# Both even output projections ahead of the odd layer, with its normed rows kept in memory as 16-bit parts

## The chip, the cores and the metric

The kernel runs on one core of one Trainium2 chip. The metric is the device time of one execution in microseconds; several executions are timed and their median is compared. One further execution is taken with the hardware profiler, and all rows below come from that one.

## The reference

One step of a two-layer decoder over 2048 prompt rows and 32 sample rows (8 sequences of 4), 1024 columns wide. Layer 0 ("even") runs HGRN2 and forgetting attention side by side, layer 1 ("odd") is a gated linear attention (GLA). Cut to what matters:

```python
for l in range(2):                       # even, then odd
    h = rmsnorm(x, norm[l])
    if l == 0:
        out = concat([o_hgrn, o_fox]) @ w_out_even     # each o gated by silu
    else:
        q, k, v, g, r = split(h @ w_in_odd, [512, 512, 1024, 1024, 16])
        log_f = log_sigmoid(r @ w_gate + b_gate) / 16
        o, s = gated_linear_chunked(q, k, v, log_f, s0)   # 4 heads
        out = (head_rmsnorm(o) * silu(g)) @ w_out_odd
    x = x + out
y = rmsnorm(x, final_norm)
```

So the odd layer's norm needs whole rows of x, that is all four column slices of the even output projection and the residual.

## The kernel before

The prompt is worked on in two halves of 1024 rows; half 0 also carries the 32 sample rows. The activations that TensorE reads stand in one tile, `act`: two 16-bit parts (a high part and the rest) of 1024 x 1056 numbers, columns being rows of x. Every projection multiplies three times (high by high, high by rest, rest by high: `mm3`, L549 to 553). There is only one `act`, so a half's input is written over the columns of what was there before, tile by tile as the matmuls have read them.

A projection is a list of *units* of some 256 weight columns. Each unit has four steps besides its matmuls: fetch (L329), measure, scale and split of its weights. `staged` (L1168) runs units a to b and slips the steps of the units one to three ahead between a unit's tile groups; it is `dense` in the odd phase. A unit of the output projection (`out_units`, L1756) ends each pair of tiles by adding the residual to the PSUM result on VectorE. An odd head has three units: Cv (values, and for head 0 also 16 gate columns), Cqk (queries, gate, keys) and Cg (the silu path). Cv of head 0 runs tile by tile, and for each tile it turns the gate columns on TensorE two tiles later (`flip`, L1837; `rh`, `rt` on VectorE before it, `prT` in PSUM). `lin_attn` is one head's recurrence: short matmuls in chains with VectorE and GpSimd. `mux` interleaves two generators by their stated costs.

The phase of the odd layer (`phase_odd`, L1909) runs, in order:

1. even output projection of half 0, units 0 to 3. Its rows x1 were loaded whole into SBUF (`row_tiles`) and are stored whole after unit 3 (L1784).
2. `start(0)`: while unit 3 runs, `handed` (L506) takes its tile pairs as they finish, through `norm_rows` (L460): square with sum on ScalarE (L481), reciprocal root, gain and scale (L485, L489), split into high part (L486, L490) and rest (L487, L491) in the staging tile `xhl`, and a DMA transpose of `xhl` into `act` (L498). Cv of head 0 starts behind it.
3. Cqk and Cg of head 0, then the recurrences of heads 0 to 2, each beside the units of the next head.
4. recurrence 3 beside `second()`: half 1's even outputs `yT` loaded and split into `act` (`y_to_act`, `y_pieces` L1710, split on L1730 to 1735), its output projection with residual slices loaded and stored through `xo` (L1771 to 1776), and `start(1)`: norm of half 1 from rows read back (three quarters from memory, the last columns copied from `xo` on L1931) and Cv of head 0 of half 1.
5. the same for half 1, then the odd output projections of both halves and the final norm.

All loads and stores of this phase go through SyncE's queue (SP), which takes them one after the other. The order of each engine's instructions, SP's too, is fixed when the program is built: a planner runs through the program with estimated times and puts next what is ready, so a later line can come ahead of an earlier one. `issue_after` puts instructions behind a given one on the same engine. Tiles of one tag share a number of buffers: `yr` two (8 KB a partition), `c2` four (shared by `xo`, the squares and the recurrence), weight raws `wr` three, split weights `w` three, PSUM `pj` three.

Of the kernel before, what the change touches and what calls it, by code (L numbers as in the profile page):

```python
# [8 lines left out]
F32 = mybir.dt.float32  # L9
F32R = mybir.dt.float32r  # L10
BF16 = mybir.dt.bfloat16
F16 = mybir.dt.float16
# [7 lines left out]
P = 128  # L20
# [89 lines left out]
def drain(g):  # L110
    for _ in g:
        pass
# [11 lines left out]
class Kern:  # L124
    def __init__(self, ctx, tc, ins, outs):
        self.ctx, self.tc, self.nc = ctx, tc, tc.nc
        self.i, self.o = ins, outs
        self.loaded, self.last_cols = {}, {}


    def consts(self):
# [27 lines left out]
        self.x1d = dp.tile([NTOK, D], F32, name="x1d")  # L159

# [344 lines left out]
    @staticmethod  # L505
    def handed(groups, first, last):  # L506


        for t in range(len(groups) + 1):
            c = next(last, None)  # L510
            if c:
                yield c
            if t >= 3:
                c = next(first, None)
                if c:
                    yield c
            if t < len(groups):
                groups[t][0]()
            if t:
                groups[t - 1][1]()  # L520
        yield from last
        yield from first
# [508 lines left out]
    def phase_even(self):  # L1031
# [4 lines left out]
        with pool("act", side="right") as ap, pool("w", side="right") as w0, pool("wl", side="right") as wp1, \  # L1036
# [5 lines left out]
            nrm = Pool(n0, {"th": 1, "nss": 4, "rs_t": 4, "rs_r": 4})  # L1042
            self.scales2, self.ready, self.fsc, self.logit, self.v_undo = {}, {}, {}, {}, {}
# [124 lines left out]
    def staged(self, us, a, b, beside=None, late=False):  # L1168
# [3 lines left out]
        def step(u, n):  # L1172
            if u < len(us):
                with ExitStack() as st:
                    if beside and n == 1 and u < 4:

                        st.enter_context(self.tc.issue_after(self.last_v.ins))
                    if late and n:
                        st.enter_context(self.tc.issue_after(self.last_lo.ins))
                    self.ready[u] = us[u][0][n]()  # L1180

        for j in range(a, b):
# [6 lines left out]
            if late:  # L1189
                todo = [[], [], [], [], [(j + 3, 0)], [(j + 2, 1)], [(j + 2, 2), (j + 2, 3)]]  # L1190
# [565 lines left out]
    def out_units(self, hf, layer, act, wpool, wp, pps, x2=None, done=None):  # L1756
# [4 lines left out]
        def mk(u):  # L1761
# [3 lines left out]
            def ev(ps, g, cnt, m):  # L1765
                c0 = self.ttiles(hf)[g][0]
                c = undo[-1 if m < P else 0][:m]
                if x2 is None:
# [4 lines left out]
                    if u == 3:  # L1773
                        self.last_cols[c0] = t
# [20 lines left out]
    def odd_half(self, hf, act, wpool, wp, pps, S):  # L1795
# [18 lines left out]
        def mk_v(h):  # L1814
            width = 272 if h == 0 else 256

            def run(W):
# [5 lines left out]
                def ev(ps, g, cnt, m):  # L1823
                    c = undo(f"Cv{h}")[:m]
                    if m == P:
                        nc.scalar.activation(v[h][:, g : g + cnt], ps[:, :, :256], AF.Copy, scale=c)
                    else:
                        nc.scalar.activation(vs[h], ps[:, 0, :256], AF.Copy, scale=c)
# [80 lines left out]
    def phase_odd(self):  # L1909
# [4 lines left out]
        with pool("act2", side="right") as ap, pool("w2", side="right") as w0, pool("yr2", side="right") as y0, \  # L1914
# [11 lines left out]
            def get_x1(hf):  # L1926
                def get(c0, m):
                    t = wp.tile([P, HALF + TS], F32, tag="c4", name=f"x1r{hf}{c0}")[:, :D]

                    nc.sync.dma_start(t[:m, :768], self.rows(hf, c0, m, False)[:, :768])  # L1930
                    nc.gpsimd.tensor_copy(t[:m, 768:], self.last_cols[c0 // 256 * 256][:m, c0 // P % 2])  # L1931
                    return t
                return get

# [12 lines left out]
            x1, x2 = [], []  # L1947
# [9 lines left out]
            def dense(a, b, **kw):  # L1957
                return self.staged(units, a, b, **kw)

            def layer(hf):  # L1960
                drain(dense(16 * hf + 5, 16 * hf + 7))
                for h in range(3):
                    drain(mux(lins[hf](h), LIN_O[hf], dense(16 * hf + 3 * h + 7, 16 * hf + 3 * h + 10), 66000.0))

            def start(hf, get):
                def stage():
                    t = wpool.tile([P, KT, 256], F32, tag="yr", name=f"xhl{hf}").rearrange("p k t -> p (k t)")
                    t = t.bitcast(F16).rearrange("p (j x d) -> p j x d", j=2, x=2)
                    return [t[:, 0], t[:, 1]]

                grow = self.gain_row(wp.tile([P, D], F32, tag="gn", name=f"grow{hf}"), i["norm_odd"][0], self.sx_odd)
                return self.handed(self.norm_rows(wp, act, hf, get, stage, grow),
                                   dense(16 * hf + 4, 16 * hf + 5, late=True), dense(16 * hf + 3, 16 * hf + 4))
# [13 lines left out]
            self.ready, self.sam = {}, None  # L1987
# [38 lines left out]
            drain(mux(lins[0](3), LIN3_A, second(), 130000.0))  # L2026
            layer(1)

# [23 lines left out]
            def third():  # L2052
                self.y_to_act(0, 1, act, wpool)
                yield from dense(32, 36)
# [65 lines left out]
```

## Time and profile before

| | |
|---|---|
| median of 3 executions | 2390.0 us |
| lowest, highest | 2389.28, 2394.76 us |
| the profiled execution | 2395.67 us |
| its span, first to last instruction | 2393.9 us |
| mean granted TensorE clock in it | 0.983 |
| moved by DMA in the span | 331.51 MB, mean 138 GB/s |
| read from and written to HBM | 243.88 and 71.11 MB |

The span starts with the first instruction; times in the views are microseconds from there. The even layer's projections and recurrences take the first part, the forgetting attention the second, and the odd phase begins at 1301.9. A row of the view by stretches gives, after its length, the busy time and number of instructions of each engine, the mean granted clock of TensorE, the mean busy share of the 16 DMA engines and the rate. A row of waits reads: who waited, for whom, microseconds in total, times, longest. A row of groups reads: line, engine, operation, output and inputs, shapes, count, then busy time in all and mean nanoseconds of one, then the engine's idle time just before them and what ended it. Buffer numbers are left out of names.

### The profile page before, as it was taken

What the parts mean: (1) busy time and instruction counts of PE and PEld (TensorE: products, weight loads), DVE (VectorE), ACT (ScalarE), POOL (GpSimd) and SP (SyncE); (2) the same over time, 40 slices, a digit from 0 to 9 for tenths busy, and PEclk for the clock granted to TensorE, in tenths of its full rate; (3) what the DMA queues carried; (4) which work ended last, traced back from release to release, by engine and by line L of the source; (5) the groups of instructions that cost most, each with busy time, mean ns of one, the idle gap of its engine ahead of it and who ended that gap; (6) DMA issues with size and microseconds to landing.
All of it is one profiled execution on the core that took longest, in us unless ns stands there. A gap on an engine that the chain in (4) does not pass through costs nothing. (4 is left out here: it accounts for less than half of the span.)

```text
span 2393.9 us, 58155 instructions
## 1 busy us (share of the span) xinstructions
PE 2279.4 (95%) x23124; PEld 1617.8 (68%) x23124; DVE 1409.6 (59%) x3256; ACT 1093.6 (46%) x2379; POOL 795.3 (33%) x858
## 2 busy tenths in 40 slices
PE   6999999999999989999999989999999899999998
PEld 5677668855655866655447867677678566666887
DVE  7566567435764547567666463665675445557554
ACT  5334354232433236466676354544543435545333
POOL 2233334112212235144466341432452322322223
PEclk9999999999999999999999999999999999999999
DMA  6231335855531276776865491222255712115453
GB/s 198 63 88 58 98 108 156 202 143 147 155 101 64 87 245 194 266 240 211 263 199 183 141 225 56 68 77 71 69 164 160 176 45 66 43 59 159 153 187 153
DMA packets 347906, 331.51 MB, mean 138 GB/s; under 512 B 90241, under 2 KB 291522, under 8 KB 347634
## 3 DMA queue, kind: packets, MB, share of 16 engines
q1 hardware_dynamic: 346130, 323.27, 44.4%
q8 instruction: 182, 2.98, 0.5%
q0 software_dynamic: 1504, 4.52, 0.5%
q14 instruction: 90, 0.74, 0.1%
HBM read 243.88 MB, written 71.11 MB: 132 GB/s over the span
## 5 line engine op out<-in xcount | busy, mean ns | idle before, releaser
L553 PE MATMUL pt_o<-w_o,act 128*128 128x256 f16 x1024 | 282.0, 275 | 4.1 <-DVE act L1735 4.1
L551 PE MATMUL pt_o<-w_o,act 128*128 128x256 f16 x1024 | 282.2, 276 | 1.4 <-ACT sg1C L607 1.4
L552 PE MATMUL pt_o<-w_o,act 128*128 128x256 f16 x1024 | 281.9, 275 | 1.4 <-POOL w_o L355 1.4
L551 PEld LDWEIGHTS <-act 128*128 128x128 f16 x2304 | 228.3, 99 | 44.0 <-issue 6.5
L553 PEld LDWEIGHTS <-act 128*128 128x128 f16 x2304 | 228.2, 99 | 39.3 <-DVE act L1735 4.9
L552 PEld LDWEIGHTS <-act 128*128 128x128 f16 x2304 | 228.3, 99 | 33.3 <-issue 2.1
L551 PE MATMUL pt_Cv<-w_Cv,act 128*128 128x256 f16 (+1 forms) x512 | 144.0, 281 | 7.8 <-DMA act<-xhl 4.1
L552 PE MATMUL pt_Cv<-w_Cv,act 128*128 128x256 f16 (+1 forms) x512 | 143.9, 281 | 0.0
L553 PE MATMUL pt_Cv<-w_Cv,act 128*128 128x256 f16 (+1 forms) x512 | 143.9, 281 | 0.0
L717 POOL TENSOR_TENSOR kA<-kA,fA 128x512 f32<-128x512 f32 (+1 forms) x56 | 79.6, 1421 | 186.8 <-PE gl_A L683 138.3
L1343 ACT ACTIVATE L<-L,nm,kc 128x512 f32<-128x512 f32 (+3 forms) x160 | 118.2, 741 | 37.3 <-DVE nm L1341 33.3
L717 POOL TENSOR_TENSOR kC<-kC,fC 128x512 f32<-128x512 f32 (+1 forms) x56 | 81.5, 1455 | 151.2 <-PE gl_C L683 105.6
L1351 POOL TENSOR_SCALAR L<-L,nm 128x512 f32<-128x512 f32 (+3 forms) x160 | 99.2, 635 | 62.8 <-DVE nm L1347 22.1
L1378 ACT ACTIVATE th<-pt 128x512 f16<-128x512 f32 (+3 forms) x159 | 80.4, 527 | 62.0 <-PE pt L1371 61.1
L1379 DVE TENSOR_TENSOR tl<-pt,th 128x512 f16<-128x512 f32 (+3 forms) x159 | 94.6, 609 | 22.3 <-ACT th L1378 21.3
L1371 PE MATMUL pt<-ident,L 128*128 128x128 f32 x544 | 92.2, 282 | 6.5 <-POOL L L1351 3.7
L1371 PEld LDWEIGHTS pt<-ident,L 128*128 128x128 f32 x544 | 67.6, 145 | 33.4 <-DVE tl L1379 8.9
L1495 PEld LDWEIGHTS pkt<-ident,pgcache_fox_k 128*128 128x128 f32 x512 | 58.3, 143 | 43.2 <-issue 25.9
L1495 PE MATMUL pkt<-ident,pgcache_fox_k 128*128 128x128 f32 x512 | 75.9, 281 | 6.7 <-DVE kts L1499 4.6
L551 PE MATMUL pt_Av<-w_Ai,act 128*128 128x256 f16 x256 | 71.1, 278 | 0.5 <-ACT act L546 0.5
L552 PE MATMUL pt_Av<-w_Ai,act 128*128 128x256 f16 x256 | 70.8, 277 | 0.4 <-DVE w_Ai L348 0.4
L553 PE MATMUL pt_Av<-w_Ai,act 128*128 128x256 f16 x256 | 71.0, 277 | 0.0
(965 smaller groups left out, 6691.9 us busy)
## 6 DMA issues: line engine op xcount, KB each, us to landing
pgcache_fox_k<-in_cache_fox_k SPq DMA_DIRECT2D x128, 256.0 KB, 4.2
pgcache_fox_v<-in_cache_fox_v SPq DMA_DIRECT2D x128, 256.0 KB, 4.0
yr<-yT SPq DMA_DIRECT2D x16, 1024.0 KB, 5.9
wr_Aqf<-in_w_in_even SPq DMA_DIRECT2D x64, 128.0 KB, 3.7
wr_o<-in_w_out_even SPq DMA_DIRECT2D x32, 256.0 KB, 4.1
wr_Cv<-in_w_in_odd SPq DMA_DIRECT2D x32, 256.0 KB, 3.4
wr_Cqk<-in_w_in_odd SPq DMA_DIRECT2D x64, 128.0 KB, 2.4
wr_Cg<-in_w_in_odd SPq DMA_DIRECT2D x32, 256.0 KB, 4.3
```

Of the source, the lines that this page charges most:

```text
L551: nc.tensor.matmul(ps, lh[0], rh[0], start=first, stop=False)
L552: nc.tensor.matmul(ps, lh[0], rh[1], start=False, stop=False)
L553: return nc.tensor.matmul(ps, lh[1], rh[0], start=False, stop=last)
L717: nc.gpsimd.tensor_tensor(kv[:, :, 0], kv[:, :, 0], t1.to_broadcast([P, nb, w]), ALU.mult)
L1343: self.last_exp = nc.scalar.activation(lt[:, :w], lt[:, :w], AF.Exp, bias=nm[:, 0:1], scale=ib, accum_out=nm[:, 2 + j : 3 + j])
L1351: nc.gpsimd.tensor_scalar(lt[:, :w], lt[:, :w], nm[:, 1:2], 2.0**14, ALU.mult, ALU.mult)
L1371: nc.tensor.transpose(pt[:, w : w + P], rows[b][s // 4][0][:, (s % 4) * P : (s % 4 + 1) * P], self.ident)
L1378: nc.scalar.activation(th[:, a:w], pt[:, a:w], AF.Copy),
L1379: nc.vector.tensor_tensor(tl[:, a:w], pt[:, a:w], th[:, a:w], ALU.subtract)))
L1495: nc.tensor.transpose(pk[:, j * P : (j + 1) * P], pgs[j][:, h * P : (h + 1) * P], self.ident)
```

## The change

The four units of half 1's even output projection move from the middle of the odd phase to right behind those of half 0; the units are renumbered (0 to 3 and 4 to 7 the even output projections, 8 to 19 the odd layer of half 0, 20 to 31 that of half 1, then 32 to 39). Both now add the residual in slices (`xo`). Half 1's `yT` is split into `act` behind unit 3, with its first two loads ahead of that unit.

The norm becomes a stream of its own, `norm_store`: rows are read back from x1d, squared, multiplied by the gain, split, and the two 16-bit parts are stored to a new tensor in memory, `xs`, of 2080 rows of 2048 numbers. Half 0's runs beside units 4 to 7, half 1's beside recurrences 0 to 2. `norm_fetch` then transposes `xs` by DMA into `act`, the sample tile first, right before Cv of head 0 of each half. The weights of the unit three ahead are fetched just before it, and `staged` leaves that fetch out later (`early`). Recurrence 3 of half 0 runs beside head 0 of half 1. The weight steps of `staged` are put behind the last eviction of Cv of head 0 on ScalarE (`last_ev`), where `late` put them behind the last rest part. `third()` loads the first two pieces of y ahead of its splits.

```diff
+        self.xs = dp.tile([NTOK, 2 * D], F16, name="xs")
...
+    def norm_store(self, pool, hf, tiles, gain):
+        todo = self.few_first(self.ttiles(hf))
+        fly = {}
+        def load(x):
+            c0, n = todo[x]
+            fly[x] = [y[:n] for y in tiles(c0)]
+            dc = T if c0 >= HALF else hf * HALF + c0
+            nc.sync.dma_start(fly[x][0], self.x1d[dc : dc + n])
+        def norm(x):
+            (c0, n), xt = todo[x], fly[x][0]
...
+            nc.scalar.activation(sq[:n], xt, AF.Square, accum_out=ss[:n])
+            fly[x].append(self.rstd(pool, ss[:n], [n, 1], D, f"n{c0}"))
+            nc.gpsimd.tensor_tensor(xt, xt, gain[:n], ALU.mult)
+        def split(x):
+            (c0, n), (xt, t, r) = todo[x], fly.pop(x)
...
+            nc.scalar.activation(t[:, 0], xt, AF.Copy, scale=r)
+            nc.vector.scalar_tensor_tensor(t[:, 1], xt, r, t[:, 0], ALU.mult, ALU.subtract)
+            nc.sync.dma_start(self.xs[dc : dc + n], t.rearrange("p x d -> p (x d)"))
+        for x in range(len(todo) + 2):
+            if x > 1:
+                split(x - 2)
+            if x < len(todo):
+                load(x)
+            if 0 < x <= len(todo):
+                norm(x - 1)
+            yield 1000
+
+    def norm_fetch(self, act, hf):
...
+        for c0, n in self.few_first(self.ttiles(hf)):
+            dc = T if c0 >= HALF else hf * HALF + c0
+            self.nc.sync.dma_start_transpose(act.both[:, :, :, c0 : c0 + n].rearrange("p x k t -> p (x k) t"),
+                                             self.xs[dc : dc + n])
...
-    def staged(self, us, a, b, beside=None, late=False):
+    def staged(self, us, a, b, beside=None):
-            if u < len(us):
+            if u < len(us) and (n or u not in self.early):
...
-                    if late and n:
-                        st.enter_context(self.tc.issue_after(self.last_lo.ins))
+                    if self.last_ev is not None:
+                        st.enter_context(self.tc.issue_after(self.last_ev.ins))
...
-                nc.sync.dma_start(t[:m, :768], self.rows(hf, c0, m, False)[:, :768])
-                nc.gpsimd.tensor_copy(t[:m, 768:], self.last_cols[c0 // 256 * 256][:m, c0 // P % 2])
...
             for hf in range(2):
-                units += self.out_units(hf, 0, act, wpool, wp, pps, None if hf else x1)
+                units += self.out_units(hf, 0, act, wpool, wp, pps)
+            for hf in range(2):
                 us, lin = self.odd_half(hf, act, wpool, wp, pps, S)
...
-            x1 += row_tiles(0, True, self.last_load)
             with tc.issue_after(self.last_y.ins):
                 drain(dense(0, 3))
-            drain(start(0, lambda c0, n: x1[c0 // P]))
-            layer(0)
-            def second():
-                self.y_to_act(1, 0, act, wpool)
-                yield from dense(16, 19)
-                yield from start(1, get_x1(1))
-            drain(mux(lins[0](3), LIN3_A, second(), 130000.0))
-            layer(1)
+            grow = self.gain_row(wp.tile([P, D], F32, tag="gn", name="grow"), i["norm_odd"][0], self.sx_odd)
+            pieces = load(self.y_pieces(1, 0, act, wpool))
+            drain(dense(3, 4))
+            split(pieces)
+            def prep(hf):
+                def tiles(c0):
+                    t = wpool.tile([P, KT, 256], F32, tag="yr", name=f"x1r{hf}{c0}").rearrange("p k t -> p (k t)")
+                    return t[:, :D], t[:, D:].bitcast(F16).rearrange("p (x d) -> p x d", x=2)
+                return self.norm_store(wp, hf, tiles, grow)
+            drain(mux(prep(0), 11500.0, dense(4, 8), 84000.0))
+            fetched(11)
+            self.norm_fetch(act, 0)
+            drain(dense(8, 11))
+            drain(mux(prep(1), 10000.0, three(0, 11), 240000.0))
+            fetched(23)
+            self.norm_fetch(act, 1)
+            drain(recur(0, 3, 20))
+            drain(three(1, 23))
```

`three(hf, a)` runs recurrences 0 to 2 of a half, each beside three units from a on; `recur` is one of them; `fetched(u)` issues the weight fetch of unit u and notes it in `early`; `load` and `split` here issue the first two loads of the pieces of y, and the splits with the remaining loads.

More of the change, by code (lines that the diff above doesn't have):

```diff
@@ L127, in __init__ @@
         self.i, self.o = ins, outs
-        self.loaded, self.last_cols = {}, {}
+        self.loaded = {}
     def consts(self):
@@ L2052, in third @@
             def third():
-                self.y_to_act(0, 1, act, wpool)
+                pieces = load(self.y_pieces(0, 1, act, wpool))
+                self.sam = None
+                split(pieces)
                 yield from dense(32, 36)
```

71 lines of the change are left out of this document (31 added, 40 removed).

## The prediction

> **What bounds the kernel now.** First the page's head: TensorE (PE) is busy in 95% of the span, so a gain can only be time in which it waits or runs slowly.
>
> ```profile
> span 2393.9 us, 58155 instructions
> PE 2279.4 (95%) x23124; PEld 1617.8 (68%) x23124; DVE 1409.6 (59%) x3256; ACT 1093.6 (46%) x2379; POOL 795.3 (33%) x858
> ```
>
> Then the sums over stretches. The bounds are where the first matmul of a stage starts. In order: even output projection of half 0, its first unit alone, the first odd unit (Cv0) of half 0, the rest of head 0, heads 1 to 3 beside recurrences 0 to 2, then in one stretch recurrence 3, the even output projection of half 1 and Cv0 of half 1, then the rest of that head, heads 1 to 3 of half 1, and all that follows.
>
> ```profile
> core 0: us, PE busy (x) PEld busy (x) DVE busy (x) ACT busy (x) POOL busy (x), PEclk, DMA share, GB/s
> 1301.90:1390.20 88.30, 86.91 (x843) 76.40 (x840) 38.78 (x69) 39.72 (x70) 30.73 (x25) 1.00 0.60 191
> 1301.90:1323.00 21.10, 21.10 (x199) 18.74 (x200) 8.45 (x17) 13.55 (x27) 6.96 (x8) 1.00 1.05 368
> 1390.20:1429.30 39.10, 30.33 (x254) 22.48 (x255) 25.45 (x55) 19.55 (x32) 16.40 (x11) 0.90 1.02 229
> 1429.30:1475.40 46.10, 45.14 (x356) 29.27 (x353) 13.25 (x23) 26.05 (x44) 5.46 (x4) 0.98 0.26 75
> 1475.40:1746.40 271.00, 262.24 (x3183) 196.31 (x3182) 167.11 (x328) 134.23 (x298) 100.69 (x85) 1.00 0.24 74
> 1746.40:1898.30 151.90, 136.81 (x1458) 114.19 (x1457) 93.43 (x167) 59.74 (x122) 60.72 (x56) 0.94 0.63 176
> 1898.30:1941.50 43.20, 42.90 (x260) 19.86 (x258) 10.99 (x15) 21.82 (x31) 5.44 (x4) 1.00 0.19 54
> 1941.50:2184.80 243.30, 240.62 (x2661) 160.71 (x2652) 133.89 (x257) 121.03 (x255) 71.41 (x63) 1.00 0.20 63
> ```
>
> A unit alone takes 21.1 us with PE busy throughout. Two stretches fall off: 39.1 us for one unit at a granted clock of 0.90, and the 151.9 us at 0.94. Both hold a handoff from the even output projection to the odd layer. What PE waited for in the two:
>
> ```profile
> PE pt_Cv L551 <- DMA act<-xhl: 3.3, 1, 3.3
> PE prT L1839 <- DVE rt L1835: 3.0, 1, 3.0
> PE pS_Cv L595 <- DVE sam_Cv L590: 2.0, 1, 2.0
> ```
>
> ```profile
> PE pt_Cv L551 <- DVE rh L1833: 3.2, 1, 3.2
> PE prT L1839 <- DVE rt L1835: 3.0, 2, 1.9
> PE st_C L551 <- ACT vp_C L788: 2.2, 1, 2.2
> PE gl_C L683 <- DVE qC L637: 2.0, 1, 2.0
> PE prT L1839 <- DVE rst_n L405: 1.9, 1, 1.9
> PE gl_C L683 <- DVE qC L716: 1.8, 1, 1.8
> ```
>
> The norm of the last rows, its split and its DMA transposes stand between the last even matmul and the first odd one, and the norm's work on DVE delays Cv0's own small steps. Each wait is followed by a stretch of slow clock, which is why the clock column falls: 0.10 of 39.1 us is 3.9 us, 0.06 of 151.9 us is 9.1 us.
>
> **The work without the waits.** I rebuild both stretches from undisturbed durations. Cv0 has the 192 matmuls of an output unit with 272 columns for 256: 21.1 x 272/256 = 22.4 us. It also turns its small gate columns on PE, once a tile:
>
> ```profile
> L1839 PE MATMUL prT<-ident,rt 128*80 128x128 f32 x15 | 4.5, 301 | 8.0 <-DVE rt L1835 6.0 <-DVE rst_n L405 1.9
> ```
>
> Nine of 0.30 us are 2.7 us. A group of sample rows is some 0.8 us (88.3 less four times 21.1 leaves 3.9 us for three groups and two short waits); two lie in the first stretch, and I allow 1 us for the next unit's first matmuls, which already run there. So 22.4 + 2.7 + 1.6 + 1 = 27.7 us of 39.1: **11.4 us to gain**.
>
> Recurrence 3: a head beside a recurrence takes 271.0/3 = 90.3 us, its matmuls alone 21.1 + 0.8 + 46.1 + 1 = 69.0, so the recurrence adds 21.3 us. After the change the 151.9 us become four output units alone, 84.4 us, and recurrence 3 beside head 0 of half 1: 21.3 + 22.4 + eight turns, 2.4, with the other 43.2 us unchanged. 84.4 + 46.1 = 130.5: **21.4 us to gain**. Together 32.8 us.
>
> **What the change adds.** (1) Between the two output projections half 1's y is split into `act` columns that unit 3 is still reading. The trace has this seam once, between the odd output projections (2295.5 on), where PE waited for the low parts and then ran at half clock for 3.4 us:
>
> ```profile
> PE pt_o L553 <- DVE act L1735: 4.1, 3, 1.8
> ```
>
> ```profile
> 2311.90:2315.30 3.40, 3.14 (x15) 2.24 (x16) 3.40 (x5) 1.05 (x5) 1.85 (x2) 0.51 0.47 161
> ```
>
> That is 4.1 + 1.7 = 5.8 us. The new seam has its first two loads issued a unit earlier and some subtractions on POOL, so it may cost nothing; I take 5.8, the only row. Bounds 0 and 5.8.
>
> The Trainium skill ("TensorE: Matmul & The Clock Gate", Part 1) says that the clock falls after at least one idle window of about 3.4 us. This trace does not agree: three waits of at most 1.8 us each brought a half-clock stretch. By the rule the seam would cost 4.1 us and the forecast would be 1.7 us lower.
>
> (2) The norm of each tile of half 0 now runs beside units 4 to 7, that of half 1 beside recurrences 0 to 2. A tile costs, from these rows:
>
> ```profile
> L481 ACT ACTIVATE nsq<-x1r 128x1024 bf16<-128x1024 f32 x8 | 8.4, 1045 | 1.7 <-POOL x1r L1931 1.7
> L489 POOL TENSOR_TENSOR x1r<-x1r,grow 128x1024 f32<-128x1024 f32 x4 | 9.8, 2453 | 5.4 <-ACT nsq L481 5.4
> L490 ACT ACTIVATE xhl<-x1r,rsr_n 128x1024 f16<-128x1024 f32 x4 | 4.6, 1149 | 8.5 <-POOL rsr_n L407 8.5
> L491 DVE SCALAR_TENSOR_TENSOR xhl<-x1r,rsr_n,xhl 128x1024 f16<-128x1024 f32 x4 | 5.1, 1276 | 0.0
> ```
>
> ACT 2.2, DVE 1.3, POOL 2.5 us. Beside units 4 to 7 nine tiles are 20, 12 and 22 us in 84 us on engines that the first unit above uses for 7 to 14 us of its 21: hidden. Uncovered, a tile's chain would be 1.0 + 2.5 + 1.1 + 1.3 us and a memory round trip. Beside the recurrences it is some 4, 6 and 7 us a head. The third head already carries about 5 more on each of the three than the second:
>
> ```profile
> 1565.70:1655.80 90.10, 87.40 (x1070) 65.47 (x1060) 54.01 (x108) 43.44 (x98) 31.80 (x27) 1.00 0.23 72
> 1655.80:1746.40 90.60, 87.48 (x1069) 65.46 (x1062) 59.03 (x112) 47.55 (x104) 37.05 (x31) 1.00 0.26 79
> ```
>
> Its time is 0.4 us over the mean of the other two, (271.0 - 90.6)/2 = 90.2. So 0.4 a head, 1.2 us. Bounds 0 and 9.4: the three waits of recurrence 3 above (2.2, 2.0, 1.8) and two slow stretches of 1.7, all within one head.
>
> (3) Cv0 of half 1 now runs inside recurrence 3, whose DVE and PSUM work its turns share. Nearest are the waits for `rt`, 3.0 us; those for the norm's `rst_n` and for `rh` behind it go. I take 3.0; bounds 0 and all three, 3.2 + 3.0 + 1.9 = 8.1.
>
> (4) DMA and SP's queue. Half 0's rows go from nine whole loads and stores to 20 slices each way, which half 1 already does; 22 further issues of 0.4 us, some 9 us of SP. In units 4 to 7 run 4.2 MB each of weights, residual loads, residual stores, row loads and split stores, and 2 MB of y: 23 MB in 84 us, 276 GB/s. The row at 1301.90 shows 368 GB/s with PE never idle, so this hides too. A new wait: with two `yr` buffers the load of tile x waits in SP's queue for the store of tile x-2. Behind it stand weight fetches and residual slices; DVE's evictions wait for those, and PE two groups (10.5 us) later, through PSUM. Split and store take about 1.1 + 1.3 + 3.2 us, within the 7.3 us (84000/11500) that the mux gives a tile: nothing.
>
> ```profile
> yr<-yT SPq DMA_DIRECT2D x16, 1024.0 KB, 5.9
> ...
> x1d<-xo SPq DMA_DIRECT2D x32, 256.0 KB, 3.2
> ```
>
> (5) The transposes: their number stays, their source becomes memory.
>
> ```profile
> L498 SPq DMA_TRANSPOSE act<-xhl x9: 1282/2086/4762, 1386.1 to 1419.2; - x9
> DMA to landing us min/median/max: 4.3/4.4/5.8
> ```
>
> Unit 7 frees two tiles of `act` every 5.3 us, so the first can start 15.8 us before its end; Cv0 eats a tile in about 3.0 us. At a pace of 2.1 us the transposes stay ahead. In half 1 unit Cg3 reads `act` in three column blocks, twice, so the first two tiles come free after 4/6 of its 26 us, some 8.7 us ahead.
>
> ```profile
> L551 PE MATMUL pf_C03g<-act,w_Cg x48: 312/313/323, 1719.8 to 1745.1; 128*128 128x352 f16 x48
> ```
>
> No row has a memory source; bounds are the pace 2.1 and 7.1 us, the longest landing of any transpose; I take 2.1, as the queue works the same way.
>
> (6) What goes without a price: the copies of the last columns on POOL, the second gain row, the ordering behind `last_lo`. What comes without one: weights of units 11 and 23 fetched a step early, weight splits ordered behind Cv0's evictions on ACT, the y loads of the third seam a little earlier. They shift work that PE does not await at a DMA share near 0.2; a wait of some 2 us either way stays inside the range.
>
> **Sum.** -32.8 + 5.8 + 1.2 + 3.0 = -22.8 us. The profiled execution took 2395.7 us (1.8 beyond its span), so 2372.9; the shown median is 5.7 lower at 2390.0, so **2367.2 us**. With every added cost at nothing 2357; at its upper bounds (5.8 + 9.4 + 8.1) 2381.
>
> **Rivals.** *A: the transposes come no earlier.* SP runs a fixed order. The last stores of unit 7 wait for its end; if the transposes stand behind them the lead is gone. Then PE waits for the sample tile's issue and a landing, 1.3 + 4.4, plus 1.7 of slow clock, and in half 1 for 4.4 + 1.7: 13.5 us, **2381**, at the edge of what can be told. For it: SP already sits long on one entry.
>
> ```profile
> SPq L329 <- DVE w_Cqk L348: 45.9, 5, 22.0
> ```
>
> Against it: the planner orders by readiness, not by text. The second gain row, written after all of half 0, was issued before that half's last transpose:
>
> ```profile
> 1416.28 0.97 SPq L456 DMA_DIRECT2D grow<-in_norm_odd  x1
> 1418.74 0.37 SPq L1721 DMA_DIRECT2D yr<-yT  x1
> 1419.20 1.28 SPq L498 DMA_TRANSPOSE act<-xhl  x1
> ```
>
> *B, slower: transposes out of memory are slow.* At a pace p half 0 has 15.8 + 21 us for 8.5 tiles, 4.3 each, half 1 8.7 + 21 for eight, 3.7; beyond that PE loses 8.5 (p - 4.3) + 8 (p - 3.7). It turns to slower (+30 us over the forecast) at p = 5.8; at 7.1 it is **2418**. For it: no memory source in the trace, and seven-microsecond landings exist. Against: ordinary loads of twice the size (`yr`) land from memory in 5.9 us.
>
> The Trainium skill ("DMA: Bandwidth & Descriptors", Latency and other measured facts) gives transposing DMAs 261 GB/s, an estimate of 2.0 us for 0.5 MB; the 2.1 us median above agrees for SBUF sources, and no run here shows memory ones.
>
> *C: the recurrences of half 0 are disturbed.* If each of half 1's eight gain multiplies (2.45 us) falls before a POOL step of the chain that PE awaits, and each wait costs 1.7 of clock: 33 us in place of 1.2, **2399**. Against: PE is busy 87.5 of 90.6 us in the loaded third head.
>
> **Chances.** Forecast 0.63, A 0.10, B 0.13, C 0.14. A measurement tells 0.3%, 7.2 us: faster is below 2382.8, slower above 2397.2. The forecast and half of A are faster (0.68), half of A and half of C no change (0.12), B and half of C slower (0.20). The range: 2355 (every cost nothing and a little over) to 2399, C's end; B stays out. The likeliest case alone spans 2357 to 2381.
>
> **What would show it.** Cv0 of half 0 in about 27 us and of half 1 in about 30 beside its recurrence, at clock near 1.00; unit 4 starting within 6 us of unit 3's end; transposes issued before unit 7 ends, from `xs`, about 2 us each; heads 1 to 3 of half 0 still 90 to 91 us. Wrong would be: a PE wait for `act<-xs` of several us, a pace above 4 us, or waits for `kC` and `qC` growing beside the norms.

## The result, and the profile after

The change makes the kernel slightly faster: 2386.47 us (median of 20 executions, 2379.19 to 2392.28) against 2392.64 us for the kernel before in the same session (20 executions, 2385.54 to 2401.83). The ratio is 0.9975, 95% interval 0.9965 to 0.9986, so 6.2 us are gained where 22.8 were forecast; 0.26% is under what the prediction called a change that can be told (0.3%). 2386.47 lies within the range, but 19 us above the predicted time and 5 us above 2381, the end of what the likeliest case alone was said to span. The kernel before ran at 2391 to 2397 us in the sessions that follow, so kernels are compared by ratios. (A ratio is an estimate of its own with its interval; the quotient of two medians differs from it by up to 0.0013.) The profiled execution of after took 2385.88 us.

The head of after's page and the sums over stretches. The bounds are again the first matmul of each stage: units 0 to 3 (even output projection of half 0), units 4 to 7 (half 1), head 0 of half 0 with its Cv0, heads 1 to 3 beside recurrences 0 to 2, recurrence 3 beside head 0 of half 1, heads 1 to 3 of half 1, all that follows.

```profile
span 2384.2 us, 58245 instructions
PE 2273.3 (95%) x23124; PEld 1617.0 (68%) x23124; DVE 1397.2 (59%) x3231; ACT 1092.9 (46%) x2379; POOL 815.8 (34%) x858
```

```profile
core 0: us, PE busy (x) PEld busy (x) DVE busy (x) ACT busy (x) POOL busy (x), PEclk, DMA share, GB/s
1305.90:1398.40 92.50, 89.24 (x869) 77.43 (x867) 37.28 (x52) 42.68 (x76) 30.94 (x25) 0.98 0.76 240
1398.40:1497.20 98.80, 89.51 (x773) 77.61 (x770) 40.23 (x51) 34.77 (x52) 43.93 (x29) 0.95 0.74 220
1497.20:1571.30 74.10, 70.86 (x583) 50.04 (x581) 21.01 (x56) 35.75 (x62) 7.36 (x6) 0.98 0.51 127
1571.30:1845.00 273.70, 262.77 (x3184) 196.86 (x3181) 184.49 (x340) 142.24 (x310) 127.29 (x97) 0.99 0.33 99
1845.00:1932.80 87.80, 85.11 (x882) 55.24 (x880) 55.61 (x131) 43.26 (x95) 30.57 (x28) 1.00 0.50 127
1932.80:2176.70 243.90, 241.85 (x2720) 161.64 (x2718) 134.35 (x260) 122.58 (x257) 71.89 (x63) 1.00 0.20 64
2176.70:2384.20 207.50, 191.82 (x2157) 168.04 (x2155) 117.92 (x230) 78.80 (x196) 60.27 (x67) 0.98 0.50 170
```

Beside the forecast, us (the forecast's column is the prediction's terms put stage by stage):

| stage | forecast | after | difference |
|---|---|---|---|
| units 0 to 3 | 88.3 | 92.5 | +4.2 |
| seam before unit 4 | 5.8 | 0 | -5.8 |
| units 4 to 7 | 84.4 | 98.8 | **+14.4** |
| head 0 of half 0: 27.7 + 46.1 | 73.8 | 74.1 | +0.3 |
| heads 1 to 3: 271.0 + 1.2 | 272.2 | 273.7 | +1.5 |
| recurrence 3 with head 0 of half 1: 21.3 + 22.4 + 2.4 + 43.2 + 3.0 | 92.3 | 87.8 | -4.5 |
| heads 1 to 3 of half 1 | 243.3 | 243.9 | +0.6 |
| the rest | 209.1 | 207.5 | -1.6 |
| odd phase | 1069.2 | 1078.3 | +9.1 |

The +9.1 is a balance: the rows above their forecast exceed it by 21.0 us in all, the rows below it stay 11.9 under.

The odd phase begins at 1305.9 instead of 1301.9, in which the even layer's instructions are the same. So the profiled executions differ by -22.8 + 9.1 + 4.0 = -9.7 us, as they do (2395.67 to 2385.88). The medians differ by only 6.2 because the profiled execution of before lies 3.0 us above its kernel's median and that of after 0.6 us below; the last run below takes this up.

One stage stands out. What PE waited for in units 0 to 3 and in units 4 to 7:

```profile
PE pt_o L583 <- ACT act L1762: 1.5, 1, 1.5
PE pS_o L627 <- DVE sam_o L622: 1.1, 1, 1.1
PE pt_o L585 <- POOL act L1763: 0.6, 1, 0.6
```

```profile
PE pt_o L583 <- DVE xo L1803: 9.2, 3, 3.5
```

L1803 is VectorE's eviction of a tile pair: PSUM plus residual into `xo`. Three times PE finds no free PSUM buffer, for 9.2 us together (3.5, 2.8 and 2.9). A stretch of 3.4 us at half clock follows each; three of 1.7 us of loss are 5.1, and 9.2 + 5.1 = 14.3 is the whole of the 14.4. Rows of the same view, one us long each, show the clock as PE resumes from the first wait, two us later, and after the second and third wait:

```profile
1444.00:1445.00 1.00, 0.76 (x7) 0.70 (x8) 0.18 (x1) 0.00 (x0) 1.00 (x1) 1.00 0.58 183
1446.00:1447.00 1.00, 1.00 (x6) 0.73 (x5) 0.00 (x0) 0.41 (x1) 0.56 (x2) 0.50 0.97 331
1467.00:1468.00 1.00, 1.00 (x7) 0.69 (x6) 0.00 (x0) 0.00 (x0) 0.00 (x0) 0.50 0.89 164
1487.00:1488.00 1.00, 1.00 (x6) 0.75 (x5) 1.00 (x2) 0.00 (x0) 0.00 (x0) 0.50 1.02 247
```

Why VectorE evicts late is read from the waits of SP, VectorE and ScalarE in units 4 to 7:

```profile
SPq L536 <- DVE x1r L535: 16.6, 6, 4.4
SPq L1802 <- ACT nsq L527: 16.3, 7, 4.6
SPq L521 <- DMA xs<-x1r: 9.7, 4, 2.9
```

```profile
DVE x1r L535 <- ACT x1r L534: 21.0, 8, 4.0
DVE rst_n L406 <- ACT nsq L527: 19.9, 8, 3.9
```

```profile
ACT nsq L527 <- DMA x1r<-x1d: 18.9, 6, 5.0
```

L521 is the read-back of a norm tile, L527 its square, L535 its rest part, L536 its store; L1802 is the load of a residual slice. The first row says that the queue stands at a store until the rest part is there, the third that the read of a tile waits for the store of the tile two before, whose buffer it takes. The second says that the residual slices wait for squares: both live in the four `c2` buffers. VectorE's two rows say that it, which works in order, stands in the norm's steps before the evictions that come behind them; ScalarE's row says that the squares wait for the reads. VectorE's list shows it at PE's three waits, which end at 1444.2, 1464.6 and 1485.0:

```profile
1443.32 0.15 DVE L406 TENSOR_SCALAR rst_n<-nss 128x1 f32<-128x1 f32 x1 [3.58 <-ACT nsq L527]
1443.43 0.75 DVE L1803 SCALAR_TENSOR_TENSOR xo<-pt_o,kc,xo 128x512 f32<-128x512 f32 x1
...
1460.41 3.50 DVE L349 SCALAR_TENSOR_TENSOR w_Cv<-wr_Cv,kc,w_Cv 128x544 f16<-128x544 f32 x2 [1.03 <-ACT w_Cv L348]
1463.84 0.74 DVE L1803 SCALAR_TENSOR_TENSOR xo<-pt_o,kc,xo 128x512 f32<-128x512 f32 x1
...
1483.02 1.28 DVE L535 SCALAR_TENSOR_TENSOR x1r<-x1r,rsr_n 128x1024 f16<-128x1024 f32 x1 [4.01 <-ACT x1r L534]
1484.22 0.75 DVE L1803 SCALAR_TENSOR_TENSOR xo<-pt_o,kc,xo 128x512 f32<-128x512 f32 x1
```

The first eviction stands behind a root that waited 3.6 us for its square, the third behind a rest part that waited 4.0 us for ScalarE. The second stands behind a weight step of 3.5 us; ScalarE did its share of that step behind a square that had waited 2.4 us for its read.

One turn of a buffer, from SP's list:

```profile
1435.59 0.39 SPq L521 DMA_DIRECT2D x1r<-x1d  x1
...
1449.09 0.35 SPq L536 DMA_DIRECT2D xs<-x1r  x1
...
1453.75 0.33 SPq L521 DMA_DIRECT2D x1r<-x1d  x1
```

From read to next read are 18.2 us, for two tiles, so 9.1 us a tile: nine tiles are 82 us, nearly all of the 84.4 forecast for the stage. Whether this turn is the cost, e1 asks.

What the prediction feared of the transposes did not come. They read memory at 2.5 us of SP each (the lines give shortest, median and longest). The sample tile's is issued at 1421.3, the first whole tile's 12 us ahead of Cv0 (1497.2), and PE waits for none:

```profile
L553 SPq DMA_TRANSPOSE act<-xs x9: 1290/2479/4066, 1421.3 to 1509.0; - x9
...
DMA to landing us min/median/max: 3.9/4.8/6.4
```

```profile
1485.42 4.07 SPq L553 DMA_TRANSPOSE act<-xs  x1
```

### The profile page after: what moved, and what is told of

Its sections match the earlier page's. It is cut to its first block, busy times and chain, and to the rows that moved or that the text cites. A ratio compares the mean times of both kernels' runs of the same rounds, so it can differ in the third digit from the quotient of the medians.

```text
span 2384.2 us, 58245 instructions
## 1 busy us (share of the span) xinstructions
PE 2273.3 (95%) x23124; PEld 1617.0 (68%) x23124; DVE 1397.2 (59%) x3231; ACT 1092.9 (46%) x2379; POOL 815.8 (34%) x858
## 5 line engine op out<-in xcount | busy, mean ns | idle before, releaser
L583 PE MATMUL pt_Cv<-w_Cv,act 128*128 128x256 f16 (+1 forms) x512 | 141.4, 276 | 0.0
L584 PE MATMUL pt_Cv<-w_Cv,act 128*128 128x256 f16 (+1 forms) x512 | 141.4, 276 | 0.0
L585 PE MATMUL pt_Cv<-w_Cv,act 128*128 128x256 f16 (+1 forms) x512 | 141.2, 276 | 0.0
L1382 POOL TENSOR_SCALAR L<-L,nm 128x512 f32<-128x512 f32 (+3 forms) x160 | 98.8, 631 | 63.0 <-DVE nm L1378 22.1
L1410 DVE TENSOR_TENSOR tl<-pt,th 128x512 f16<-128x512 f32 (+3 forms) x159 | 94.5, 609 | 21.4 <-ACT th L1409 20.4
L1855 ACT ACTIVATE vC<-pt_Cv,kc 128x512 f32<-128x512 f32 (+1 forms) x40 | 23.9, 599 | 123.2 <-PE pt_Cv L585 123.2
L583 PE MATMUL pt_Av<-w_Ai,act 128*128 128x256 f16 x256 | 71.1, 278 | 0.5 <-ACT act L578 0.5
L584 PE MATMUL pt_Av<-w_Ai,act 128*128 128x256 f16 x256 | 70.9, 277 | 0.4 <-DVE w_Ai L349 0.4
```

Of the source, the lines that this page charges most:

```text
L583: nc.tensor.matmul(ps, lh[0], rh[0], start=first, stop=False)
L584: nc.tensor.matmul(ps, lh[0], rh[1], start=False, stop=False)
L585: return nc.tensor.matmul(ps, lh[1], rh[0], start=False, stop=last)
L1382: nc.gpsimd.tensor_scalar(lt[:, :w], lt[:, :w], nm[:, 1:2], 2.0**14, ALU.mult, ALU.mult)
L1410: nc.vector.tensor_tensor(tl[:, a:w], pt[:, a:w], th[:, a:w], ALU.subtract)))
L1855: r = nc.scalar.activation(v[h][:, g : g + cnt], ps[:, :, :256], AF.Copy, scale=c)
```

## The experiments

Stage lengths of all kernels, us, from one trace each. "Read back" says whether half 0's norm reads its rows from memory, "c2" whether its squares take a `c2` buffer.

| kernel | read back | c2 | units 0-3 | units 4-7 | head 0 | heads 1-3 | ratio to before, interval |
|---|---|---|---|---|---|---|---|
| after | yes | yes | 92.5 | 98.8 | 74.1 | 273.7 | 0.9975 (0.9965-0.9986) |
| e1 four tile buffers | yes | yes | 92.2 | 98.6 | 71.9 | 274.4 | 0.9947 (0.9925-0.9968) |
| e2 squares out of c2 | yes | no | 92.6 | 101.8 | 91.6 | 268.4 | 1.0008 (0.9994-1.0022) |
| e3 whole rows | yes | yes | 89.5 | 102.1 | 71.8 | 274.1 | 0.9975 (0.9958-0.9991) |
| e4 without the norm | yes | none | 92.7 | 91.8 | 72.2 | 274.1 | 0.9925 (0.9903-0.9947) |
| e5 e1 and e2 | yes | no | 92.8 | 94.6 | 73.8 | 268.3 | 0.9909 (0.9885-0.9933) |
| e6 e5 and e3 | yes | no | 88.5 | 96.2 | 73.2 | 269.2 | 0.9894 (0.9867-0.9920) |
| e7 normed from SBUF | no | no | 88.9 | 86.7 | 75.4 | 268.8 | 0.9881 (0.9854-0.9908) |
| e8 off VectorE | yes | yes | 92.6 | 97.4 | 76.5 | 274.2 | 0.9970 (0.9953-0.9987) |
| e9 e7 and idle reads | unread | no | 89.4 | 88.0 | 73.7 | 269.8 | 0.9886 (0.9871-0.9900) |
| e10 SBUF, squares in c2 | no | yes | 89.4 | 97.4 | 73.4 | 273.3 | 0.9949 (0.9937-0.9962) |
| e11 ordering alone | yes | yes | 92.4 | 96.8 | 76.2 | 273.8 | 0.9977 (0.9966-0.9989) |

**e1: four buffers for half 0's tiles.** Every second tile lies in another tag's buffer, so a read waits for the store of the tile four before.

```diff
...
+    if hf == 0 and count[0] % 2 == 0:
+        t = wp.tile([P, 8, 256], F32, tag="v8", name=f"x1v{hf}{c0}").rearrange(...)
+    else:
         t = wpool.tile([P, KT, 256], F32, tag="yr", name=f"x1r{hf}{c0}").rearrange(...)
```

> Half 0's norm beside units 4 to 7 gets four tile buffers in place of two (every second tile takes one of two value buffers that are idle then). Ring theory: a tile holds one of two buffers for its load (4 to 6 us), chain (7 us) and store (4 to 5 us), some 18 us, so the norm gives a tile every 9 us where the units need one every 7.3, and VectorE's fixed order carries that into the residual evictions: with four buffers the waits of PE for xo (9.2 us) go, the four units fall from 98.8 us to 85 to 88, and the time falls by 10 to 13 us below the changed kernel (ratio to before about 0.992). Scratch theory (the squares take slots of the ring that the residual slices use, so residual loads wait for squares): within 3 us of the changed kernel. Traffic theory (DMA engines or SP's queue are full): no faster, as every transfer stays.

Units 4 to 7 stayed (98.6 for 98.8). That the two tile buffers alone hold the stage back falls, and with it that the turn of 18.2 us does so by itself. The ratio came out lower than after's, with intervals that just meet.

**e2: squares out of the c2 buffers.** The square, of which only the sum is wanted, is written over the tile of 16-bit parts.

```diff
-    sq = pool.tile([P, D], BF16, tag="th", name=f"nsq{c0}")
-    nc.scalar.activation(sq[:n], xt, AF.Square, accum_out=ss[:n])
+    nc.scalar.activation(fly[x][1][:, 0], xt, AF.Square, accum_out=ss[:n])
```

> The squares of the norm are written where the high part will stand, not into a buffer of the c2 ring. Scratch theory: PE's waits for xo (9.2 us) go, 10 us below the changed kernel. Ring theory: the norm still gives a tile every 9 us, the four units stay at 95 us or more, at most 3 us gained. Traffic theory: no change.

Units 4 to 7 did not gain (101.8), so the `c2` buffers alone are not the cause either. Two other stages moved: heads 1 to 3 fell by 5.3 us, and head 0 rose by 17.5. The second is, for the most part, one wait:

```profile
PE prT L1869 <- DVE rT L1870: 14.5, 1, 14.5
```

```profile
1508.18 0.47 ACT L1854 ACTIVATE vC<-pt_Cv,kc 128x256 f32<-128x256 f32 x1 [2.31 <-PE pt_Cv L584]
1526.43 1.06 ACT L526 ACTIVATE x1r<-x1r 128x1024 f16<-128x1024 f32 x1 [17.78 <-DMA x1r<-x1d]
```

```profile
1515.04 3.04 SPq L552 DMA_TRANSPOSE act<-xs  x1
...
1521.35 0.94 SPq L521 DMA_DIRECT2D x1r<-x1d  x2
```

In this kernel the planner's order has half 1's first square ahead of Cv0's evictions on ScalarE, and the read for it stands in SP's queue behind the transposes, which hold the queue 2 to 3 us each. VectorE's root stands 16.3 us for that square, with Cv0's small steps behind it. Variants e5, e6, e7, e9 and e11 order such squares behind Cv0's last eviction ("ordering").

**e3: half 0's residual as whole rows**, loaded and stored as before the change.

```diff
-    units += self.out_units(hf, 0, act, wpool, wp, pps)
+    units += self.out_units(hf, 0, act, wpool, wp, pps, None if hf else x1)
...
+    x1 += row_tiles(0, True, self.last_load)
```

> One part undone: half 0's residual comes as whole rows loaded ahead and stored whole, as before the change; all else as changed. If the slices cost the first projection its 4.2 us (92.5 us for units 0 to 3 against 88.3 before), it returns to about 88.3 and the time falls by 4 us below the changed kernel; units 4 to 7 stay near 98.8 under every theory. If the 4.2 us were only this execution's, no change.

Units 0 to 3 fell by 3.0 us, units 4 to 7 rose by 3.3, which no theory had expected, and the ratio stayed. In all traces units 0 to 3 take 88.5 to 89.5 with whole rows (e3, e6, e7, e9, e10) and 92.2 to 92.8 with slices (the other seven): the slices cost 3 to 4 us there. They are seen in the waits: 3.2 us for parts of y and the sample tile in after (the three rows for units 0 to 3 in the section before) and one stretch at half clock (1.7), against 1.5 us for weights and none in e3.

**e4: half 0's norm leaves out square, root and gain**; half 0's rows are only split. All transfers stay.

```diff
 def norm(x):
+    if hf == 0:
+        fly[x].append(1.0)
+        return
...
```

> Half 0's norm leaves out the square, the root and the gain: rows are loaded, split and stored, so every transfer stays and a tile's chain on the engines falls from 7 to about 2.5 us. Ring theory: (5 + 2.5 + 4.5)/2 = 6 us a tile, under 7.3, units 4 to 7 in 85 to 88 us. Scratch theory: the same, as no squares are left there. Traffic theory: units 4 to 7 stay near 98.8 us.

Units 4 to 7 fell by 7.0 us, to 91.8, which is 7.4 over the forecast's 84.4: with the reads, the split and the stores alone PE still waits there for 6.0 us. Neither the 85 to 88 of the first two theories nor the 98.8 of the third came.

**e5 and e6: both sets of buffers.** e5 joins e1 and e2 with the ordering below; e6 adds e3's whole rows.

```diff
+    with ExitStack() as st:
+        if self.last_ev is not None:
+            st.enter_context(self.tc.issue_after(self.last_ev.ins))
         nc.scalar.activation(fly[x][1][:, 0], xt, AF.Square, accum_out=ss[:n])
```

> Four tile buffers and squares outside the c2 ring together (each alone left units 4 to 7 at 98.6 and 101.8 us), and half 1's squares put behind Cv0's last eviction. Two-rings theory (the tile buffers and the c2 ring each limit, so only both together help): units 4 to 7 in 85 to 89 us, ratio to before about 0.992. Order theory (VectorE takes its instructions in a fixed order, and residual evictions stand behind steps of the norm that wait for a load from memory, whatever the rings hold): units 4 to 7 stay over 92 us, ratio 0.995 or above.

> As the run with both rings relieved, and half 0's residual as whole rows loaded ahead. Expected of it beside that run: units 0 to 3 from 92.5 to about 89 us, 3 us less in all; if the rows' stores at unit 3's end delay the read-back, as in the run with whole rows alone (102.1 us for units 4 to 7), the gain is given back there.

Together the buffers take 4.2 us off units 4 to 7 where neither did alone; the long wait of e2 is gone and the 5 us of heads 1 to 3 stay. PE still waits 8.8 us in e5's units 4 to 7, so most of the loss (10.2 of 14.4 us) has another source than the number of tile buffers and the squares' place.

**e7: no read-back.** Half 0's rows are kept whole in SBUF and normed from there; the squares are out of `c2`, the ordering stays, the tiles are the two `yr`.

```diff
-    def norm_store(self, pool, hf, tiles, gain):
+    def norm_store(self, pool, hf, tiles, gain, here=None):
...
+        if here:
+            fly[x][0] = here[c0 // P][:n]
+            return
```

> Half 0's rows are loaded whole, kept in SBUF, and normed from there: no read-back of x1 for half 0, so no step of its norm waits for a load; squares outside the c2 ring; two tile buffers as in the changed kernel. Order theory: units 4 to 7 in 85 to 88 us, since nothing that VectorE meets waits for memory, and units 0 to 3 at about 89, so 12 to 15 us below the changed kernel, ratio about 0.991. If two tile buffers alone were the limit: (7 + 4.6)/2 = 6 us a tile, also relieved. If DMA traffic or SP is the limit: 4 MB less of 23 MB, a small gain only.

```profile
1391.00:1477.70 86.70, 84.34 (x773) 75.04 (x770) 39.62 (x52) 34.72 (x52) 44.16 (x29) 1.00 0.68 213
```

```profile
PE pt_o L588 <- DVE xo L1808: 2.4, 3, 1.3
```

Units 4 to 7 take 86.7 us: the forecast's 84.4 and 2.4 of waits, at full clock. VectorE, ScalarE and GpSimd are as busy as in after, within 0.7 us, so the loss was never a matter of their load. At 0.9881 (0.9854 to 0.9908; median 2365.66 us, the kernel before 2397.18) this beats both kernels. Beside e6, which has whole rows, squares out of `c2` and ordering too, and more tile buffers, only the read-back is gone: 86.7 us for 96.2.

**e8: half 0's norm off VectorE.** Its root goes to GpSimd, its split to ScalarE and GpSimd, in after's buffers.

```diff
...
+    nc.scalar.activation(xt, xt, AF.Copy, scale=r)
+    nc.scalar.activation(t[:, 0], xt, AF.Copy)
+    nc.gpsimd.tensor_tensor(t[:, 1], xt, t[:, 0], ALU.subtract)
```

> The changed kernel with half 0's norm steps taken off VectorE (the root's first step and the rest part to GpSimd, the scaling to ScalarE); rings, loads and stores as changed. Order theory: the residual evictions no longer stand behind the norm, PE's waits for xo fall from 9.2 to under 3 us, units 4 to 7 in 86 to 90 us. Two-rings theory: residual loads still wait for squares and the tile ring is slower (a longer chain), so units 4 to 7 stay at 98 us or more.

97.4: the norm's place in VectorE's order alone is not the cause. ScalarE, in order too, stands 35.6 us before the squares, for the reads (18.9 in after), and the evictions on VectorE wait for their residual slices instead:

```profile
ACT nsq L527 <- DMA x1r<-x1d: 35.6, 7, 12.2
```

```profile
DVE xo L1808 <- DMA xo<-in_x_prompt: 50.6, 5, 16.3
```

**e9: e7 with the reads put back, unread.** The same nine loads go into a spare tile (the edit is shown against e7).

```diff
+    if x % 2 == 0:
+        spare[0] = pool.tile([P, 8, 256], F32, tag="v8", name=f"spare{x}").rearrange(...)
+    nc.sync.dma_start(spare[0][:n, x % 2 * D : x % 2 * D + D], self.x1d[dc : dc + n])
     fly[x][0] = here[c0 // P][:n]
```

> e7 (rows of half 0 normed from SBUF) with one thing added: half 0's rows are read back from memory as in the change, nine loads of 0.5 MB in SP's queue at the same places, but into a spare tile that nothing reads. The loads still wait in SP's queue for the rows' stores. Theory (the norm waits for its data: load, square, split, store in two rings, and VectorE's evictions stand behind it): units 4 to 7 stay at e7's 86.7 us, within 2, and the ratio within its interval, 0.985 to 0.991. Rival 1 (the loads' hold on SP's queue and their traffic delay the residual slices): units 4 to 7 go back to 93 us or more, ratio 0.991 or higher.

```profile
1394.20:1482.20 88.00, 84.57 (x773) 75.04 (x770) 44.18 (x52) 34.91 (x52) 47.32 (x30) 1.00 0.84 262
```

88.0 us and 0.9886: with the DMA engines at 0.84 and 262 GB/s, more than after's 0.74 and 220, PE is hardly held. Neither the traffic nor SP's time for the loads is the cost. What is left of the read-back is that the norm must wait for it.

**e10: e7 with the squares in c2 and no ordering** (against e7 again).

```diff
-    nc.scalar.activation(fly[x][1][:, 0], xt, AF.Square, accum_out=ss[:n])
+    sq = pool.tile([P, D], BF16, tag="th", name=f"nsq{c0}")
+    nc.scalar.activation(sq[:n], xt, AF.Square, accum_out=ss[:n])
```

> Only the rows of half 0 normed from SBUF (loaded and stored whole, as before the change); the squares go back to the four-slot c2 ring and no square is ordered behind Cv0's last eviction. Theory: units 4 to 7 near e7's 86.7 us (within 3), heads 1 to 3 beside recurrences 0 to 2 back at 273 to 274 us from 268.8, since there half 1's squares take c2 slots from the recurrence; ratio about 0.990 (0.988 to 0.993). Rival 1 (the squares in c2 are what delays units 4 to 7): 93 us or more there, ratio 0.993 or higher. Rival 2 (the five us beside the recurrences came from the ordering of the squares): heads 1 to 3 go to 273 too in the next run, e11, where only the ordering is added, or stay at 268 to 269 here.

The theory missed on units 4 to 7: 97.4 us, and rival 1 was right there. The waits of e10's units 4 to 7, by ScalarE, SP, VectorE and PE:

```profile
ACT nsq L530 <- DMA x1d<-xo: 14.6, 5, 6.0
ACT nsq L530 <- DMA wr_Cv<-in_w_in_odd: 10.0, 1, 10.0
```

```profile
SPq L1805 <- ACT nsq L530: 7.4, 6, 1.6
```

```profile
DVE rst_n L406 <- ACT nsq L530: 20.4, 6, 8.5
```

```profile
PE pt_o L586 <- DVE xo L1806: 10.1, 5, 7.6
```

A square waits until a finished slice has left its `c2` buffer for memory, VectorE's root waits for the square with the evictions behind it, and the next slice's load waits for the square in turn. The second row, behind which PE's longest wait (7.6 us) stands, names a load of weights, but that square started at 1459.95, as the store of a finished slice landed: issued at 1454.35, behind three weight loads in SP's queue, it took 5.4 us. The weight load named landed only after the square had begun.

**e11: the ordering alone**, added to the change (e5's lines around the square, which stays in `c2`).

> The change with one thing added: the squares of half 1 that are issued in or after Cv0 stand behind Cv0's last eviction on ScalarE. Theory: nothing in units 4 to 7 (98.8 us within 3), nothing beside the recurrences (273 to 274 us); ratio 0.996 to 0.999. Rival: the ordering gives the five us beside the recurrences (268 to 269 us), ratio about 0.9955.

96.8 and 273.8 us, ratio 0.9977: nothing in either. The 5 us in heads 1 to 3 belong to the squares, with e2, e5, e6, e7, e9 at 268.3 to 269.8 and all kernels with half 1's squares in `c2` at 273.3 to 274.4. In these seven kernels PE's `gl_C` waits once for VectorE's `qC` in heads 1 to 3, 2.7 to 2.8 us; in the other five it does not. That is a sign of being wrong that the prediction had named ("waits for `kC` and `qC` growing beside the norms").

**e12: the kernel before once more.**

> The kernel before once more, unchanged, for a second trace of it. The twelve traces of the change and its variants enter the odd phase between 1301.6 and 1308.0 us, mean 1304.6; the one trace of before at 1301.9, and its odd phase took 1092.0. Theory (the even layer, whose instructions are the same, differs from execution to execution): the odd phase begins anywhere in 1301 to 1308 and lasts 1090 to 1094. Rival (the change also lengthens the even layer, by three or four us): it begins at 1300 to 1302 again.

It took 2391.32 us. The odd phase begins at 1304.1, 2.2 us later than in the other trace of the same kernel, so its start moves in the kernel before too, and no longer even layer need be laid to the change. But the odd phase took 1085.5 us, outside what was expected. Nearly all of the 6.5 us lie in the stretch of recurrence 3, even output of half 1 and Cv0:

```profile
1749.50:1895.00 145.50, 133.18 (x1467) 112.60 (x1458) 93.23 (x167) 59.50 (x122) 61.10 (x56) 0.96 0.65 180
```

The prediction's row has 151.9 us at 0.94 for the same work, with 3.6 us more of PE busy (136.81 against 133.18), about two half-clock stretches of 1.7 us, and 2.8 us more of standing. What makes the executions differ is not shown.

## Why the prediction was wrong in its size

The direction, the two stretches to gain in, and the fate of the transposes were right. That the time lies within the range is luck: the range's upper end was made for rival C, which did not come, and 11.9 us in the stages that took less than forecast covered part of the loss. Point by point:

**The failing step: (2) and (4), the norm of half 0 beside units 4 to 7, costed at nothing.** Step (2) compared loads ("20, 12 and 22 us in 84 us ... hidden") and step (4) found "split and store ... within the 7.3 us". Both are true of the busy times, and e7 shows them harmless when nothing has to be waited for. The step left out that the norm's steps wait for memory, and that VectorE, in order, takes its evictions behind them. Of a tile's turn it measured only the end: read, square, root, gain, split and store took 18.2 us over two buffers, 9.1 a tile against the 7.3 given (though four buffers, in e1, left the stage at 98.6). And it did not see that squares and residual slices share `c2`, so that each set waits for the other. Step (4) did name a path to the evictions, but another one: residual slices that stand behind the read in SP's queue. In after VectorE waits only 0.5 us for slices; only e8, without the norm on VectorE, shows that path at length (50.6 us). The step cost 14.4 us.

The runs show that cost as a two by two, units 4 to 7 in us:

| | squares in c2 | squares elsewhere |
|---|---|---|
| rows read back | 98.8 (after), 96.8 (e11) | 101.8 (e2) |
| rows from SBUF | 97.4 (e10) | 86.7 (e7), 88.0 (e9) |

Either one brings 10 to 15 us over e7, and both together no more; taking one away gains at most 1.4. The lower row also has half 0's residual as whole rows; these do not bring the gain, as e3 and e6, with whole rows and the read-back, take 102.1 and 96.2. That the traffic is not the cost is shown by e9. In every trace with the loss PE waits for VectorE's evictions alone or for the most part (in e1, 3.3 of 9.2 us are put to a root step, in e5, 0.9 of 8.8, and in e8, 2.3 of 11.3 to a slice's load). Which link decides isn't separated: with the rows read back the squares wait for reads, with squares in `c2` for slices to leave, and in e8 the evictions wait for slices without any norm step on VectorE. Nor does the sum of VectorE's waits for squares decide, which is 19.9 us in after and 17.4 in e9, where units 4 to 7 take 1.3 us more than in e7.

```profile
DVE rst_n L406 <- ACT x1r L536: 17.4, 7, 5.2
```

A rival stays open here: the planner lays every variant's instructions anew, so VectorE's order differs between them too (after and e11 have the same one, and lose 14.4 and 12.4 us). No run kept the order and took only the waits away, so how much of the 10 to 15 us is waiting and how much is where the planner puts the evictions isn't known.

**(4), half 0's slices for whole rows: costed at nothing, 3 to 4 us** (units 0 to 3, five traces against seven). The row of 368 GB/s without PE idling, on which the step rested, was of one unit that had no slices. Why parts of y come later with slices wasn't tried.

**(1), the seam: 5.8 us, measured 0.** PE waits for no part of y before unit 4; the lower bound was right. With the first two loads ahead of unit 3 no wait was left; which part of the change saw to that wasn't tried.

**The work without the waits.** Head 0 of half 0 came out at 74.1 for 73.8, so the 11.4 us were there but for the 0.3. The 21.4 us of the other stretch were read from an execution in which it was long: by e12's row, 145.5, they are 15.0. Against that second execution the odd phase gained 1085.5 - 1078.3 = 7.2 us, and of the 22.8 us forecast 6.5 are missing from the start: 22.8 - 6.5 - 9.1 = 7.2. The medians moved by 6.2; with one trace of after and two of before, that the two agree so closely is partly chance.

**(2) for half 1, and (3).** Heads 1 to 3 rose to 273.7, 1.5 over the forecast's 272.2. The surcharge of 1.2 was sized near enough, but it hides two effects: the norm without squares in `c2` costs nothing (268.3 to 269.8 against 271.0 and 270.6 in the traces of before), the squares some 5 us. Recurrence 3 with head 0 took 87.8 to 90.1 in all twelve traces, 92.3 being forecast with step (3)'s 3.0 us: at most 0.8 of these came.

**Rivals.** A fell: the whole tiles' transposes begin 12 us before Cv0, where 15.8 were forecast. B fell: 2.5 us of SP each where 2.1 were taken, no pace near 5.8 us, and no wait of PE for them in after. C's 33 us did not come: heads 1 to 3 rose by 2.7 over before, which the squares' buffers explain and not GpSimd's multiplies, as these stay in e2, e5 to e7 and e9, which have 268.3 to 269.8. What came true, a norm that waits for memory in front of the evictions, was no rival; the nearest to it, step (4)'s "new wait", was priced at nothing.

## What to carry to other kernels

When work is moved beside a dense stage, count the whole turn of its buffers, from the load's issue to the next load into the same place, against the time that the stage gives, list who else takes buffers of the same tag, and see what stands behind the moved steps on each engine that takes its work in order; busy shares say nothing of these. More buffers for the tile alone gained nothing in its stage here (e1). If two waits can each hold back the same engine, taking one away shows nothing: try both together before either is ruled out. A gain that is read off one stretch of one execution should be read off a second execution too.

## What the runs showed of the hardware

- After a wait of 3.5 us, which ended at 1444.2, PE ran on at full clock for about a microsecond and only then at 0.50 (rows of 1444 and 1446 above). The second and third wait were 2.8 and 2.9 us, and the clock fell after both (rows of 1467 and 1487). The Trainium skill ("TensorE: Matmul & The Clock Gate", Part 1) names at least one idle window of about 3.4 us before the clock falls; as in the trace of before, shorter waits did it here. Not every such wait does: in e3 one of 2.7 us, which ended at 1447.2, was followed by five microseconds at 1.00.
- Half 0's nine transposes out of memory hold SP's queue 1.3 to 4.1 us each and land in 4.8 us (median), against 1.3 to 4.8 and 4.4 for the nine out of SBUF in the kernel before.
- Nine more reads in units 4 to 7 (eight of 0.5 MB and the sample rows), 262 GB/s for 213, made the stage only 1.3 us longer (e9 against e7).
- The same kernel's stretch of 151.9 us took 145.5 in another execution, with 2.8 us less of standing and fewer half-clock stretches.
